# Sums of weights in DRAM issued two per step, and tile pools at new addresses

## The chip, the cores and the metric

The kernel runs on one core of a Trainium2 chip. PE (TensorE) does the matmuls, ACT (ScalarE) and DVE (VectorE) the work on single elements, POOL (GpSimd) and SP (SyncE) issue most of the transfers, which 16 DMA engines carry out. The metric is the time of one execution on the device in microseconds. An execution with a profile is a single one, and its time stands in the table below beside the span that the profile shows.

## The reference

One layer of a diffusion backbone: 512 latent tokens and 256 context tokens, 1,024 channels, all in fp32.

```python
mod_lat = silu(c) @ w_ada + b_ada              # six rows: sh1, sc1, ga1, sh2, sc2, ga2
z = modulate(x, g_norm1, sh1, sc1) @ w_in + b_in
x_a, b_a, c_a, q, k, v, r, lr_f, lr_b, gate_a, gate_b = split(z)
# ... the same projection of the context gives the first state of the scans
o = gla_bidir(q, k, v, g_f, g_b, s_f, s_b)     # gated linear attention, both directions, 4 heads
y_a = (b_a * conv3(c_a * x_a)) @ w_conv_out
y_b = (rmsnorm(o) * silu(r)) @ w_gla_out
y = sigmoid(gate_a) * y_a + sigmoid(gate_b) * y_b
x = x + ga1 * (y @ w_o)
x = x + ga2 * square(relu(modulate(x, g_norm2, sh2, sc2) @ w_up)) @ w_down
return rmsnorm(x, g_final)
```

## The kernel before, in words

Every large product is taken in three parts. An operand is split into a high part `h` and a low part `l`, both kept as fp32r, and `mm3` (line 132) issues high x high, high x low and low x high into the same PSUM tile. One weight tile of 128 x 1024 numbers gives 8 x 3 = 24 matmuls of 512 columns.

`weights` (line 121) brings such a tile: SP issues the load of a raw tile `r_`, ACT copies it to `h_` (the high part), DVE subtracts to get `l_`. There are four raw tiles (`NRAW`) and five of `h_` and `l_` each (`NW`). The class `Stream` walks through a plan of all weight tiles in the order of use (v, q, xa/c/b, ga, co, r, gb, go, wo, up, dn) and keeps up to three ahead. The names in the trace follow from it: `r_co`, `h_co`, `l_co` are the weights of the product `ps_co`. Of the two operands behind the arrow in a matmul's name, the first is the moving one and the second the stationary one: in ps_v, ps_y and the down projection the weights move, in all other products the activations do.

The main loop (line 923) runs over the 57 steps of `projections`. Beside each step it advances the attention of the four heads by one piece, then the sums, and from step 44 on (`MODS_FROM`) the second modulations, which load `wa` tiles into the same raw tiles. Then come the 16 steps of `gates` (r and gb), the products go and wo, and the MLP: 32 up tiles and 7 x 8 dn tiles. The seven products of the down projection use combinations of quarters of `w_down`, in the manner of Strassen and Winograd.

These combinations are the sums that the change is about. `weight_sums` (line 458) is a generator of 64 pieces of work on POOL. Each piece is two instructions: a COPY of one number of the latest low weight part to `tick`, which holds POOL back until that split is done, and a transfer from DRAM to DRAM into a tile `t`, either a plain copy of a quarter of `w_down` or of another `t`, or an accumulation onto `t`. In the order of issue: 16 copies, 16 accumulations, 8 copies from `t`, 8 accumulations, 8 copies, 8 accumulations. The first reader of a `t` is the third product of the down projection. `SUMS` says how many are drawn after step 0, step 1 and so on, the last entry standing for all later steps.

POOL's other work in that part of the program is small: two broadcasts of a bias (`vb`), clearing `lrf` and `lpb` for each head (lines 635, 636), and clearing and loading `acc` for the modulations. POOL issues in one order, so each of these stands behind the sums drawn before it. ACT, DVE and PE also keep the order in which a scheduler puts them.

The tile pools lie behind each other in SBUF in the order in which they are opened: `const`, `wp` (raw, high and low weights), `kp` (long-lived blocks, the projections' left or right operands `hh` and `hl`, `h2h`, `h2l`), `sp` (small columns) and `bp` (blocks of 512 numbers, among them `ogh`, `ogl`, `yh`, `yl`), in whose place `mp` comes later (`aph`, `apl`).

Of the kernel before, what the change touches and what calls it, by code (L numbers as in the profile page):

```python
# [8 lines left out]
F32 = mybir.dt.float32  # L9
# [6 lines left out]
P = 128  # L16
# [23 lines left out]
NBLK = 36  # L40
NKEEP = 16
MODS_FROM = 44
SUMS = (0, 1)
UP_ORDER = [16 * j + 4 * g + i for g in range(4) for j in range(2) for i in range(4)]
TABLES = "natural_log_exp_and_others"

# [2 lines left out]
def hybrid_block_kernel(  # L49
# [9 lines left out]
    w_up, w_down, b_in, b_ada, out = w_up[0], w_down[0], b_in[0], b_ada[0], out[0]  # L59

    const = es.enter_context(tc.tile_pool(name="const", bufs=1))
    wp = es.enter_context(tc.tile_pool(name="wp", bufs=NW))
    kp = es.enter_context(tc.tile_pool(name="kp", bufs=NKEEP))
    sp = es.enter_context(tc.tile_pool(name="sp", bufs=4))
    pp = es.enter_context(tc.tile_pool(name="pp", bufs=8, space=bass.MemoryType.PSUM))
    dp = es.enter_context(tc.tile_pool(name="dp", bufs=1, space=bass.MemoryType.DRAM))

# [36 lines left out]
    def raw_tile(name):  # L104
        return wp.tile([P, 1024], F32, tag="raw", name=name, bufs=NRAW)
# [4 lines left out]
    def split(src, hi, lo):  # L110
        act.copy(out=hi, in_=src)
        dve.tensor_tensor(out=lo, in0=src, in1=hi.bitcast(F32), op=ALU.subtract)
# [6 lines left out]
    latest = [None]  # L119

    def weights(name, src):

        raw = raw_tile("r_" + name)
        a, b = src.shape[1], src.shape[2]
        nc.sync.dma_start(out=raw.rearrange("p (a b) -> p a b", a=a), in_=src)
        hi = wp.tile([P, 1024], F32R, tag="hi", name="h_" + name)
        lo = wp.tile([P, 1024], F32R, tag="lo", name="l_" + name)
        split(raw, hi, lo)
        latest[0] = lo
        return hi.rearrange("p (a b) -> p a b", a=a), lo.rearrange("p (a b) -> p a b", a=a)  # L130
# [282 lines left out]
    mod_w[1] = [ada_raw(1, q) for q in range(2)]  # L413
    normalized(x_tok, r_x, 0, P)
    wq = weights("q0", cols(w_in, C_Q))
    key_weights(1)
    Engine.ordered = False
# [32 lines left out]

    t_sum = [[dp.tile([P, 2, 512], F32, tag=f"t{i}_{p}", name=f"t{i}_{p}") for p in range(NFF // 4)] for i in range(4)]
    tick = const.tile([1, 1], F32, name="tick")

    def quarter(j, hf, p):
        return rows(w_down, 16 * j + 2 * p, 512 * hf)

    def weight_sums():

        groups = range(NFF // 4)
        todo = [(i, p, quarter(0, i, p), False) for p in groups for i in range(2)]  # L460
        todo += [(i, p, quarter(i, 1, p), True) for p in groups for i in range(2)]
        for i, j, hf in ((2, 1, 1), (3, 1, 0)):
            todo += [(i, p, t_sum[(0, 2)[i - 2]][p], False) for p in groups]
            todo += [(i, p, quarter(j, hf, p), True) for p in groups]
        for i, p, src, add in todo:
            pinned(nc.gpsimd.tensor_copy(out=tick, in_=latest[0][0:1, 0:1].bitcast(F32)))
            pinned(nc.gpsimd.dma_start(out=t_sum[i][p], in_=src, **({"accum_op": ALU.add} if add else {})))  # L467
            yield

    def down_weights(n, p):  # L470

        if n in (2, 3, 5, 6):
            return weights("dn", t_sum[{2: 0, 3: 2, 5: 1, 6: 3}[n]][p])
        return weights("dn", quarter(*{0: (1, 0), 1: (0, 0), 4: (1, 1)}[n], p))
# [300 lines left out]
    def all_attention():  # L775
        for h in range(HEADS):
            yield from attention(h)
# [3 lines left out]
    def second_mods():  # L781
        yield from ada_sum(3)
        ps = psum("ps_ac")
        for k in range(KT):
            pe.matmul(ps[:, k:k + 1], ada[3][k // 4][:, (k % 4) * P:(k % 4 + 1) * P], ones[:, 0:1], start=True, stop=True)
        dve.tensor_copy(out=sh2, in_=ps[:, 0:KT])
        yield
        yield from ada_rows(4)
        for hf in range(2):
            g2 = blk("g2")  # L790
            nc.gpsimd.dma_start(out=g2, in_=g_norm2[0][hf * 512:(hf + 1) * 512].partition_broadcast(P))
            dve.scalar_tensor_tensor(out=ada[4][hf], in0=ada[4][hf], scalar=1.0, in1=g2, op0=ALU.add, op1=ALU.mult)
        yield from ada_rows(2)
# [110 lines left out]
    def gates():  # L904

        for j in range(KT):
            ps = project("r")
            rg = blk("rg")
            pinned(act.activation(out=rg, in_=ps, func=AF.Silu, bias=cb(40 + j)))
            pst = transposed("ps_ot", o_tok, j)  # L910
            dve.scalar_tensor_tensor(out=rg, in0=pst, scalar=ca(80 + j), in1=rg, op0=ALU.mult, op1=ALU.mult)
            og.append((blk(f"ogh_{j}", F32R), blk(f"ogl_{j}", F32R)))
            split(rg, *og[j])
            yield
        for j in range(KT):
            ps = project("gb")
            gb.append(kblk("gb"))
            pinned(act.activation(out=gb[j], in_=ps, func=AF.Sigmoid, bias=cb(56 + j)))
            yield
        pinned(nc.scalar.preload_act_table_set(TABLES))  # L920

    att, mods, sums = all_attention(), second_mods(), weight_sums()
    for i, _ in enumerate(projections()):
        next(att, None)
        for _ in range(SUMS[min(i, len(SUMS) - 1)]):
            next(sums, None)
# [3 lines left out]
        next(mods, None)  # L930
    for _ in gates():
        next(mods, None)
        next(sums, None)
    for _ in mods:
        pass
    for _ in sums:
# [291 lines left out]
```

## Time and profile before

| | |
|---|---|
| median of 3 runs | 1000.24 us (999.66 to 1001.4) |
| the profiled execution | 1002.8 us, span 1001.0 us |
| mean granted clock of PE | 0.989 of 2.4 GHz |
| PE busy | 963.0 us, 96% |
| DVE, ACT, POOL busy | 637.0, 487.8, 109.2 us |
| chain that ended last | PE 90%, DMA 4%, DVE 3% |
| DMA queue q1 (SP's and others' loads) | 41.4% of 16 engines, 123.89 MB |
| DMA queue q0 (POOL's transfers) | 15.1% of 16 engines, 35.43 MB |

The page gives for each engine the time in which it executed something, and the chain of waits follows the work that ended last back to its beginning. A matmul's shown duration overlaps the next one's; how fast PE works is therefore read from the starts, or from a piece of the chain (so many microseconds for so many matmuls without a break). The granted clock is 1.00 at 2.4 GHz and 0.50 at 1.2 GHz.

### The profile page before, as it was taken

To read this page: it belongs to the slowest core of one execution; us is meant where nothing else is said; L and a number is where in the kernel's file an instruction comes from. 1 tells how busy PE (TensorE), PEld (TensorE's weight loads), DVE (VectorE), ACT (ScalarE), POOL (GpSimd) and SP (SyncE) were. 2 spreads that over 40 slices of the span, in tenths; PEclk is the share of its full clock that TensorE was granted. 3 is DMA by queue.
4 is the path that set the end of the run, shared out by engine and by line. 5 is a ranking of instruction groups with operands and counts; after the bars stand their busy time and mean duration, and the time that the engine had idled before them with its cause. 6 is when DMAs were issued, how large, how long until landed. Compare 5 with 4: busy or idle time off the path is not lost.

```text
span 1001.0 us, 13478 instructions
## 1 busy us (share of the span) xinstructions
PE 963.0 (96%) x4999; PEld 783.9 (78%) x4999; DVE 637.0 (64%) x1076; ACT 487.8 (49%) x862; POOL 109.2 (11%) x195
## 2 busy tenths in 40 slices
PE   3999999999999998799989999999999999999996
PEld 2678888778888887688878888898888888888875
DVE  5366676887688767666547354776332225699896
ACT  4465454645655474533334432374444344655662
POOL 7001021222211131002220000000000000000000
PEclk9999999999999999899989999999999999999998
DMA  9893154787664666855987425237533334555561
GB/s 264 231 289 127 33 190 138 164 169 164 144 167 146 172 129 154 244 169 175 251 205 235 129 98 171 61 89 234 162 85 105 95 116 142 192 179 191 179 211 42
DMA packets 160241, 161.22 MB, mean 161 GB/s; under 512 B 7268, under 2 KB 126160, under 8 KB 159920
## 3 DMA queue, kind: packets, MB, share of 16 engines
q1 hardware_dynamic: 146672, 123.89, 41.4%
q0 software_dynamic: 12928, 35.43, 15.1%
q10 hardware_dynamic: 576, 1.05, 0.3%
q8 instruction: 39, 0.64, 0.3%
q14 instruction: 26, 0.21, 0.1%
HBM read 158.25 MB, written 35.65 MB: 194 GB/s over the span
## 4 chain that ended last, share of the span: by engine, by line
PE 90%; DMA 4%; DVE 3%; SPq 1%; ACT 1%; issue 1%; DVEq 0%; ACTq 0%
PE ps_up L81 16%; PE ps_da L81 7%; PE ps_v L81 7%; PE ps_b L81 4%; PE ps_y L81 4%; PE ps_c L81 4%; PE ps_db L81 4%; PE ps_go L81 4%; PE ps_xa L81 4%; PE ps_gb L81 4%; PE ps_co L81 4%; PE ps_r L81 4%; PE ps_ga L81 2%; PE ps_dc L81 2%; DMA r_co<-in_w_conv_out_dram 2%; PE ps_k L81 2%
## 5 line engine op out<-in xcount | busy, mean ns | idle before, releaser
L81 DVE TENSOR_TENSOR l_up<-r_up,h_up 128x1024 fp32r<-128x1024 f32 x32 | 39.2, 1224 | 84.8 <-ACT h_up L81 84.7
L81 PE MATMUL ps_up<-h2h,l_up 128*128 128x512 f32 x232 | 90.3, 389 | 0.0
L81 PE MATMUL ps_up<-h2l,h_up 128*128 128x512 f32 x232 | 90.3, 389 | 0.0
L81 PE MATMUL ps_up<-h2h,h_up 128*128 128x512 f32 x232 | 90.3, 389 | 0.0
L81 DVE TENSOR_TENSOR l_dn<-r_dn,h_dn 128x1024 fp32r<-128x1024 f32 x56 | 68.4, 1222 | 27.1 <-ACT h_dn L81 26.9
L81 ACT CAST h_up<-r_up 128x1024 fp32r<-128x1024 f32 x32 | 33.6, 1053 | 78.8 <-PE ps_up L81 67.9
L81 ACT CAST h_dn<-r_dn 128x1024 fp32r<-128x1024 f32 x56 | 58.7, 1048 | 16.1 <-PE ps_up L81 16.1
L81 ACT CAST aph<-ug 128x512 fp32r<-128x512 f32 x56 | 34.8, 621 | 58.8 <-PE ps_da L81 25.6
L81 DVE SCALAR_TENSOR_TENSOR acc<-wa,silu_c,acc 128x512 f32<-128x512 f32 x64 | 45.4, 747 | 8.4 <-DMA wa<-in_w_ada_dram 8.2
L81 PEld LDWEIGHTS ps_up<-h2l,h_up 128*128 128x128 f32 x232 | 43.5, 188 | 9.1
L81 PEld LDWEIGHTS ps_up<-h2h,l_up 128*128 128x128 f32 x232 | 43.5, 188 | 9.0
L81 PEld LDWEIGHTS ps_up<-h2h,h_up 128*128 128x128 f32 x232 | 43.5, 188 | 9.0
L81 DVE TENSOR_TENSOR apl<-ug,aph 128x512 fp32r<-128x512 f32 x56 | 38.6, 689 | 13.5 <-ACT aph L81 13.2
L467 POOL DMA_DIRECT2D t<-in_w_down_dram x48 | 42.7, 905 | 3.8 <-issue 3.8
L81 PE MATMUL ps_da<-h_dn,aph 128*128 128x512 f32 x96 | 37.9, 395 | 0.0
L81 PE MATMUL ps_da<-h_dn,apl 128*128 128x512 f32 x96 | 37.9, 395 | 0.0
L81 PE MATMUL ps_da<-l_dn,aph 128*128 128x512 f32 x96 | 37.9, 394 | 0.0
L81 PE MATMUL ps_co<-yah,h_co 128*128 128x512 f32 x64 | 26.5, 413 | 0.0
L81 PE MATMUL ps_r<-hh,h_r 128*128 128x512 f32 x64 | 26.4, 412 | 0.0
L81 PE MATMUL ps_v<-h_v,hh 128*128 128x512 f32 x64 | 26.0, 406 | 0.0
L81 PE MATMUL ps_r<-hh,l_r 128*128 128x512 f32 x64 | 25.8, 402 | 0.0
L81 PE MATMUL ps_r<-hl,h_r 128*128 128x512 f32 x64 | 25.7, 401 | 0.0
(464 smaller groups left out, 2794.5 us busy)
## 6 DMA issues: line engine op xcount, KB each, us to landing
t<-in_w_down_dram POOLq DMA_DIRECT2D x48, 512.0 KB, 7.6
wa<-in_w_ada_dram SPq DMA_DIRECT2D x32, 512.0 KB, 4.8
r_up<-in_w_up_dram SPq DMA_DIRECT2D x32, 512.0 KB, 4.1
r_dn<-t SPq DMA_DIRECT2D x32, 512.0 KB, 3.5
r_dn<-in_w_down_dram SPq DMA_DIRECT2D x24, 512.0 KB, 3.6
wa<-in_w_ada_dram SPq DMA_DIRECT2D x32, 256.0 KB, 5.1
t<-t POOLq DMA_DIRECT2D x16, 512.0 KB, 5.3
r_v<-in_w_in_dram SPq DMA_DIRECT2D x8, 512.0 KB, 5.2
```

What stands on the lines that cost most here:

```text
L81: ins = op(*args, **kwargs)
L467: pinned(nc.gpsimd.dma_start(out=t_sum[i][p], in_=src, **({"accum_op": ALU.add} if add else {})))
```

## The change

`SUMS` becomes (0, 1, 2): no sum after step 0, one after step 1, two after each later step until none is left. The loop over `gates` no longer draws any. The pool `sp` is opened before `wp`, a tile of 24 numbers at the end of `const` moves all later pools by 96 bytes, and a tile of 16 numbers (64 bytes) is put once between the high and the low weight parts. Everything else in the program stays, apart from line numbers.

```diff
-SUMS = (0, 1)
+PAD = 24
+SUMS = (0, 1, 2)
...
     const = es.enter_context(tc.tile_pool(name="const", bufs=1))
+    sp = es.enter_context(tc.tile_pool(name="sp", bufs=4))
     wp = es.enter_context(tc.tile_pool(name="wp", bufs=NW))
     kp = es.enter_context(tc.tile_pool(name="kp", bufs=NKEEP))
-    sp = es.enter_context(tc.tile_pool(name="sp", bufs=4))
...
         hi = wp.tile([P, 1024], F32R, tag="hi", name="h_" + name)
+        if latest[0] is None:
+            wp.tile([P, 16], F32, tag="gap", name="gap", bufs=1)
         lo = wp.tile([P, 1024], F32R, tag="lo", name="l_" + name)
...
     tick = const.tile([1, 1], F32, name="tick")
+    const.tile([P, PAD], F32, name="pad")
...
     for _ in gates():
         next(mods, None)
-        next(sums, None)
```

In the built programs the tiles start at these places, given as the address within a partition modulo 256 bytes (all the tiles concerned are multiples of 256 bytes long, so those of one kind share the place):

| | before | after |
|---|---|---|
| raw and high weights (`r_`, `h_`) | 32 | 0 |
| low weights (`l_`) | 32 | 64 |
| `kp` (`hh`, `hl`, `h2h`, `h2l`, ...) | 32 | 64 |
| `bp`, `mp` (`yah`, `ogh`, `yh`, `aph`, ...) | 160 | 64 |

Counted over the matmuls of 512 columns (without a few of the modulations), by the distance of the places of their two operands: before, 2,280 at distance 0 (v, q, xa, c, b, ga, r, gb, up) and 1,284 at 128 (co, go, y, the seven products of the down projection, k); after, about 1,252 at 0 and 2,312 at 64, two in three of nearly every stage, since `h_` is an operand of two of the three parts and `l_` of one.

On POOL, around the first tick on l_c, where the projections xa, c and b begin, the order was this (COPY is the tick, DMA the sum; the tile's first number is its place among the eight of a group):

```order
L466 COPY tick<-l_q 1x1
L467 DMA t_5_695<-in_w_down_dram 256x1x512
L466 COPY tick<-l_c 1x1
L467 DMA t_6_688<-in_w_down_dram 256x1x512
L635 MEMSET lrf 128x512
L636 MEMSET lpb 128x512
L466 COPY tick<-l_b 1x1
L467 DMA t_6_696<-in_w_down_dram 256x1x512
L466 COPY tick<-l_xa 1x1
L467 DMA t_7_689<-in_w_down_dram 256x1x512
```

Now the same place on POOL reads:

```order
L470 COPY tick<-l_c 1x1
L471 DMA t_3_694<-in_w_down_dram 256x1x512
L470 COPY tick<-l_c 1x1
L471 DMA t_4_687<-in_w_down_dram 256x1x512
L639 MEMSET lrf 128x512
L640 MEMSET lpb 128x512
L470 COPY tick<-l_b 1x1
L471 DMA t_4_695<-in_w_down_dram 256x1x512
L470 COPY tick<-l_b 1x1
L471 DMA t_5_688<-in_w_down_dram 256x1x512
L470 COPY tick<-l_xa 1x1
L471 DMA t_5_696<-in_w_down_dram 256x1x512
```

Each split now lets two sums go, and the clearing of `lrf` and `lpb` stands behind one more of them; 23 sums lie ahead of the first tick on l_c, where 12 did, so the 24th, an accumulation, stands where the 13th, a copy, stood.

Later on POOL, where the loads of ga give way to those of co and the second modulations start (`acc`), the order was:

```order
L751 DMA acc0_3831<-in_b_ada_dram 1x16x32
L751 DMA acc1_3832<-in_b_ada_dram 1x16x32
L466 COPY tick_714<-l_ga_3844 1x1
L467 DMA t2_4_702<-in_w_down_dram 256x1x512
L466 COPY tick_714<-l_co_3920 1x1
L467 DMA t2_5_703<-in_w_down_dram 256x1x512
L466 COPY tick_714<-l_co_3995 1x1
L467 DMA t2_6_704<-in_w_down_dram 256x1x512
```

Now the last sums on POOL stand on splits of xa and c, and `acc` comes after all of them:

```order
L470 COPY tick_715<-l_xa_3052 1x1
L471 DMA t3_6_713<-in_w_down_dram 256x1x512
L470 COPY tick_715<-l_c_3124 1x1
L471 DMA t3_7_714<-in_w_down_dram 256x1x512
L639 MEMSET lrf_3716 128x512
L640 MEMSET lpb_3717 128x512
L754 MEMSET acc0_3873 128x512
L754 MEMSET acc1_3874 128x512
L755 DMA acc0_3873<-in_b_ada_dram 1x16x32
```

No sum is left for the steps of ga, co, r and gb. On PE, DVE, ACT and SP the order is the same, row by row, as before.

## Rows read from the trace of the kernel before

**Rows 1.** The page's busy times, whole span

```profile
PE 963.0 (96%) x4999; PEld 783.9 (78%) x4999; DVE 637.0 (64%) x1076; ACT 487.8 (49%) x862; POOL 109.2 (11%) x195
```

**Rows 2.** Chain of waits, pieces at ps_gb, ps_go, ps_up (start us, us, what)

```profile
524.97 35.13 PE ps_gb L81 x155
...
569.99 35.09 PE ps_go L81 x151
...
689.84 40.35 PE ps_up L81 x178
```

**Rows 3.** PE's timeline in the ps_go steps (start us, us, what)

```profile
570.28 0.40 PE L81 MATMUL ps_go<-ogl,h_go 128*128 128x512 f32 x1
570.52 0.40 PE L81 MATMUL ps_go<-ogh,l_go 128*128 128x512 f32 x1
```

**Rows 4.** PE's timeline around 415 us (idle before and its releaser in brackets)

```profile
414.67 1.12 PE L81 MATMUL ps_sl<-qt,kt 128*64 128x64 f32 x16 [5.01 <-DVE kt L81]
...
416.32 0.63 PE L81 MATMUL ps_co<-yal,h_co 128*128 128x512 f32 x1
...
418.02 0.63 PE L81 MATMUL ps_co<-yah,l_co 128*128 128x512 f32 x1
```

**Rows 5.** PE's timeline, three more starts after idle time

```profile
386.44 0.69 PE L81 MATMUL ps_sl<-qt,kt 128*64 128x64 f32 x16 [1.76 <-DVE kt L81]
...
388.72 0.58 PE L81 MATMUL ps_s<-vcl,kwh 128*128 128x256 f32 x1 [1.28 <-DVE vcl L81]
...
504.65 0.80 PE L81 MATMUL ps_ar<-ah,ones_r 128*128 128x512 f32 x1 [2.81 <-ACT ah L81]
```

**Rows 6.** Windows: first and last of three stretches, PEclk before DMA share

```profile
388.15:391.56 3.41, 2.84 (x12) 2.84 (x13) 3.41 (x8) 1.15 (x5) 0.00 (x0) 0.50 0.24 65
...
504.20:511.03 6.83, 6.37 (x14) 4.70 (x15) 1.80 (x3) 0.92 (x2) 0.89 (x1) 0.50 1.10 278
```

**Rows 7.** The chain of waits, 370 to 420 us

```profile
374.10 8.63 DMA r_co<-in_w_conv_out_dram
...
397.49 13.14 DMA r_co<-in_w_conv_out_dram
```

**Rows 8.** DMA issues of the page, KB each, median us to landing

```profile
r_ga<-in_w_in_dram SPq DMA_DIRECT2D x8, 512.0 KB, 4.5
```

**Rows 9.** DMA queues of the whole span: packets, MB, share of 16 engines

```profile
q1 hardware_dynamic: 146672, 123.89, 41.4%
q0 software_dynamic: 12928, 35.43, 15.1%
```

**Rows 10.** DMA queues, 180 to 290 us

```profile
q0 software_dynamic: 4083, 7.87, 43.4%
q1 hardware_dynamic: 16438, 8.29, 27.5%
```

**Rows 11.** DMA queue q0 and its issues, 472 to 516 us

```profile
q0 software_dynamic: 2128, 4.20, 50.2%
...
t<-in_w_down_dram POOLq DMA_DIRECT2D x8, 512.0 KB, 9.8
```

**Rows 12.** Windows: an early stretch, DMA share before GB/s

```profile
92.00:164.00 72.00, 72.00 (x478) 60.71 (x477) 47.92 (x99) 30.41 (x68) 7.55 (x13) 1.00 0.24 78
```

**Rows 13.** POOL and DVE timelines: two ticks, vb, lrf and their first readers

```profile
124.09 0.60 POOL L827 DMA_DIRECT2D vb<-in_b_in_dram  x1
...
164.43 1.04 POOL L466 COPY tick<-l_c 1x1 f32<-1x1 f32 x1 [30.32 <-DVE l_c L81]
...
165.96 0.55 POOL L635 MEMSET lrf<- 128x512 f32 x1
...
292.04 0.17 POOL L466 COPY tick<-l_c 1x1 f32<-1x1 f32 x1 [3.43 <-DVE l_c L81]
...
132.29 0.69 DVE L81 TENSOR_TENSOR v<-ps_v,vb 128x512 f32<-128x512 f32 x1
...
177.02 0.42 DVE L81 TENSOR_TENSOR lrf<-lrf,lpf 128x256 f32<-128x256 f32 x1
```

## The prediction

> **What bounds the kernel now.** I read the page's busy times first. PE is busy for 963.0 of 1001.0 us and no other engine for more than 637.0 [rows 1], so the time is the sum of what PE executes, how fast matmul follows matmul, and the few places where PE stands still. I then took these two apart, because the change touches both, one with its DRAM sums and the other with its addresses.
>
> The speed of the stream is read in long unbroken pieces of the chain of waits. At ps_gb 155 matmuls take 35.13 us, 226.6 ns each; at ps_up 178 take 40.35 us, 226.7 ns each; at ps_go 151 take 35.09 us, 232.4 ns each [rows 2]. All are 512 columns wide at full clock. What sets ps_go apart in the table of addresses is that its two operands stand 128 bytes apart modulo 256, while those of ps_gb and ps_up stand at the same place. In ps_go single distances reach 240 ns, between the starts at 570.28 and 570.52 [rows 3]. At half clock four distances take 1.70 us, 425 ns each [rows 4], so half of that, some 213 ns, is what 512 columns would take at full clock with nothing lost between them.
>
> The idle places are read on PE's timeline. From 20 to 970 us only four idle spells exceed 1 us: 1.76 and 1.28 us before 386.44 and 388.72, 5.01 us before 414.67 and 2.81 us before 504.65 [rows 4, 5], in all 10.86 us. PE waits there for DVE or ACT, but neither is the cause. The chain goes back from them to r_co, which takes 8.63 and 13.14 us to land [rows 7]; ACT, which splits weights and serves attention in one fixed order, stands before h_co and everything behind it stands too. The load r_ga, of equal size, lands in a median of 4.5 us [rows 8]. Beside the stalls the granted clock falls to 0.50 in three stretches of 3.41 to 6.83 us [rows 6]. In that state a matmul takes 427 instead of 232 ns. Seven matmuls in the second stretch and 14 in the third lose some 0.195 us each, 4.1 us; of the first, 3.41 us long, at most half is lost, 1.7. That makes 5.8 us.
>
> **The change part by part.** First the sums. Nothing is added: the same 64 copies and accumulations run, and PE, DVE, ACT and SP keep their order word for word. Only POOL's order changes. From the second projection step on each step issues two, so of 64 the last comes in about the 33rd step, near 292 us by the times of before, and none in the steps of co, r and gb. DMA q0 spends 15.1% of 1001.0 us on some 64 transfers [rows 9], 2.36 us of all 16 engines each, and in 472 to 516 us, where eight accumulations stand, 50.2% [rows 11]. There they share the engines with the loads of r and gb. If that is what makes r_co and r_gb late, the loads come nearer to the 4.5 us of r_ga, the four spells and the clock behind them go, and 10.86 + 5.8 = 16.7 us are gained. What is late next is the ring of four raw buffers, which the modulation weights (wa) share from step 44 on; that stays, and I leave 2.7 us to it. I take −14 us; the bounds are 0 and −16.7.
>
> The cost of the sums where they go: between 180 and 290 us q0 and q1 already take 43.4% and 27.5% [rows 10]. The last 41 sums will stand on the 21 ticks from l_c at 164.43 to l_c at 292.04 [rows 13], 41 × 2.36 = 97 us of transfer, and with 27.5% of these 127.6 us, 35 us, for the loads: 132 us of transfer in 128 us. The loads of that stretch are issued some 20 us ahead of their split, and that queue ahead hides a delay of 5 to 10 us per load; I cost it at nothing. Without that cover it is rival 4. The sums on l_v and l_q, 23 instead of 12, fall in or before a stretch of 72 us with a DMA share of 0.24 [rows 12], where 55 us are free for 11 × 2.36 = 26 us more; also nothing. Behind the longer first burst stand the second vb and, two sums further back each time, the memsets of lrf and lpb. Vb is issued at 124.09 and read from 132.29 on; lrf is cleared at 165.96 and read at 177.02 [rows 13]. One or two sums more in front (about 1 us of POOL's issue each) fit into 8 and 11 us, so nothing here either.
>
> Second the addresses. Of 3,564 wide products 2,280 had both operands at the same place modulo 256 and 1,284 were 128 apart; now about 1,252 are at the same place and 2,312 are 64 apart. No product of the kernel before is 64 apart, so the price is bounded. From below it is 213 ns, the bare columns; from above 240 ns, the longest single distance of ps_go [rows 3]; the rows nearest on either side, at distances 0 and 128, are 226.7 and 232.4 ns. I take 226.7, because 64 is nearer to a full match in phase than the half period, where single distances swing; this is the weakest choice of the sum. With it the 1,284 lose 5.7 ns each, −7.3 us. Each nanosecond of error on the 2,312 is worth 2.3 us, so the ends are 2,312 × (213 − 226.7) − 7.3 = −39 us and 2,312 × (240 − 226.7) − 7.3 = +23 us.
>
> The sum: the profiled execution took 1002.8 us, 1.8 more than its span. 1002.8 − 14 − 7.3 = 981.5 us. The median of the runs shown is 1000.24, 2.56 lower, which makes 979 us.
>
> **The rivals.** (1) Distance costs as such: the 2,312 products run at the 232.4 ns of ps_go. For it speaks that this is the only unequal distance that a row shows. Against it, that 128 is the farthest that two places can be. Then (2,312 − 1,284) × 5.7 = +5.9 us stand against −14: 992 us.
>
> (2) The lost time between matmuls is a meeting of two readers at the same place, and 64 bytes apart they don't meet. For it: 226.7 is 14 ns above the bare columns even where nothing waits. Against: at 128 apart it got worse. At 213 ns it gives 2,312 × −13.7 − 7.3 = −39 us, with the sums 947 us. The Trainium skill has a gap of its own for this ("TensorE: Matmul & The Clock Gate", section "Back-to-back issue gap"): a matmul of 512 columns follows the last after 518 cycles, 216 ns. The trace doesn't agree, at 226.6 and 232.4 ns [rows 2]; by the page's figure on the 2,312 this rival would read 954 us.
>
> (3) Addresses don't matter to PE, and ps_go is slower for another reason, its left operand's age or DVE's traffic say. Then only the sums count, −14 us: 986 us. The Trainium skill says so: in "SBUF — State Buffer", section "Who interferes with whom", PE has two independent read ports and never waits on anyone. Against it stand two products of the same shape, engine and clock that differ by 5.8 ns [rows 2].
>
> (4) The moved sums starve the loads. An accumulation costs more than the mean: 50.2% of 44 us for eight is 2.8 us [rows 11]. A load costs 41.4% of 1001.0 us × 0.52 of 123.89 MB, 1.75 us [rows 9]. Two accumulations and a load take 7.35 us, a step takes 127.6 us / 21 = 6.1, and over 12 steps with accumulations 15 us are short. Uncovered, that and a clock spell of some 2 us return as stalls: 979 + 17 = 996 us. Against it: the loads' lead is longer than that.
>
> (5) The co and r loads are late from the raw ring and the wa loads, not the sums. For it: r_co at 374.10 is issued only when its buffer falls free. Against: its 8.63 us from issue to landing are past that point [rows 7]. Half of the stalls stay: 986 us.
>
> (6) The slower side: 64 apart, every distance is as long as the longest of ps_go. One mechanism, a clash of the two operand streams in 2,312 products, at 240 ns: +23 − 14 = 1009 us. It decides from the pitch at which 2,312 × (p − 226.7) exceeds 14 + 7.3, that is 235.9 ns. For it: 128 showed that a distance can cost, and nothing bounds it at 64. Against: even ps_go averages 232.4.
>
> **How the numbers follow.** Forecast (973 to 985 us) 0.40; rival 1 0.13; rival 2 0.15; rival 3 0.08; rival 4 0.07; rival 5 0.06; rival 6 0.11. The predicted time is 979 us. Rival 2 reaches to 947 and I leave out its lower half; rivals 1 and 4 can end near 1000, and of rival 6 the lower part is taken in: 950 to 1003 us. A measurement of this kernel can't tell 0.2%, 2 us, from no change. Slower by more: rival 6 and a little of rivals 1 and 4, 0.14. Within: 0.08 from the edges of the same. Faster: 0.78.
>
> **What would show it.** In the changed profile: no idle spell of PE over 1 us between 380 and 510 us, granted clock 1.00 throughout that stretch, r_co and r_gb landing in 4 to 6 us, and no `t` issue by POOL after some 300 us. The sums term is wrong if idle spells stay at co and gb, or new ones stand between 160 and 300 us behind r_xa, r_c or r_b. The address term is read in the pieces of ps_gb, ps_go and ps_up: about 227 ns in all three is the forecast, 232 rival 1, under 220 rival 2, unchanged by stage rival 3, 236 and more rival 6. The prediction is wrong as a whole if the long pieces' pitch lies outside 222 to 230 ns.

## The result and the profile after

The changed kernel takes 995.52 us (median of 19 runs, 994.3 to 1000.83) against 1001.45 us for the kernel before (19 runs, 999.06 to 1006.05). The ratio is 0.994, with a 95% interval of 0.9928 to 0.9953. That is 6 us faster; I had forecast 979 us, a gain of 21 us; the range of 950 to 1003 us holds the time.

The profiled execution took 1000.83 us, the longest of the 19, with a span of 999.1 us. The page of the changed kernel, with the line of busy times, the granted clock in 40 slices, and the chain by engine:

```profile
PE 966.6 (97%) x4999; PEld 780.7 (78%) x4999; DVE 637.3 (64%) x1076; ACT 487.8 (49%) x862; POOL 107.5 (11%) x195
...
PEclk9999999989999999999999999999999999999999
...
PE 87%; DMA 7%; DVE 3%; ACT 1%; SPq 1%; issue 1%; POOL 0%; DVEq 0%; ACTq 0%; POOLq 0%
```

PE is busy 3.6 us longer than before [rows 1] although the span is shorter, and the ninth slice of the clock has an 8: the loss sits elsewhere now.

First the stretch of co, r and gb. This is the DMA view from 370 to 420 us: queues (packets, MB, share of 16 engines), then the issues of r_co with their median time to landing.

```profile
q1 hardware_dynamic: 8362, 6.93, 46.4%
...
q0 software_dynamic: 64, 0.00, 0.1%
...
r_co<-in_w_conv_out_dram SPq DMA_DIRECT2D x8, 512.0 KB, 4.0
```

The same view of the kernel before:

```profile
q0 software_dynamic: 1216, 3.15, 31.0%
...
r_co<-in_w_conv_out_dram SPq DMA_DIRECT2D x7, 512.0 KB, 8.6
```

The sums are gone from q0, and r_co lands in a median of 4.0 us, where before it was 8.6 and two of its loads took 8.63 and 13.14 us [rows 7]. The four idle spells of [rows 4, 5] have no counterpart, and the clock stays at 1.00 from 220 to 995 us.

Second, the chain of waits near 214 us (start us, us, what), and the timelines of ACT and PE behind it:

```profile
178.12 32.50 DMA r_c<-in_w_in_dram
...
210.70 1.05 ACT h_c L82
...
211.83 1.23 DVE l_c L82
...
213.66 0.62 DVE kt L82
...
214.42 1.12 PE ps_sl L82 x16
```

```profile
210.70 1.04 ACT L82 CAST h_c<-r_c 128x1024 fp32r<-128x1024 f32 x1 [10.87 <-DMA r_c<-in_w_in_dram]
```

```profile
214.42 1.12 PE L82 MATMUL ps_sl<-qt,kt 128*64 128x64 f32 x16 [4.21 <-DVE kt L82]
```

A load of r_c, issued at 178.12, takes 32.50 us to land. ACT stands before h_c for it for 10.87 us, DVE behind ACT, and PE has nothing to do for 4.21 us until kt is there. It is the same chain of events as the stall at co before, 200 us earlier. The windows view shows what follows (the clock stands before the DMA share), and beside it the whole stretch of the doubled sums; the DMA queues of that stretch come behind.

```profile
213.55:220.38 6.83, 5.96 (x28) 4.82 (x29) 6.83 (x14) 3.37 (x8) 3.70 (x7) 0.50 0.83 267
164.00:290.00 126.00, 121.28 (x673) 97.53 (x671) 91.39 (x171) 68.71 (x139) 50.15 (x80) 0.97 0.94 230
```

```profile
q0 software_dynamic: 5917, 18.82, 62.7%
q1 hardware_dynamic: 19919, 10.04, 30.9%
```

The clock is at 0.50 for 6.83 us, and q0 and q1 together take 93.6% of the engines from 164 to 290 us, with 62.7% for the sums. Before they took 43.4% and 27.5% in nearly the same stretch [rows 10]. How the two queues share the engines while r_c is under way is seen from 178 to 186 us:

```profile
q0 software_dynamic: 696, 1.34, 90.4%
q1 hardware_dynamic: 696, 0.35, 21.6%
```

Both moved the same number of packets, 696, but those of the loads are much smaller, so SP's queue got 0.35 MB in 8 us. At that rate one load of 512 KB takes some 12 us (an estimate from these two lines), and several were waiting: the loads of r_b and r_xa that follow took 26.7 and 21.6 us. With the old addresses (sums_only, 174 to 182 us) the counts are 701 and 699.

Third, the speed of the stream, from pieces of the chain at gb, go and the down projection, and behind them the down projection of the kernel before:

```profile
524.94 35.25 PE ps_gb L82 x154
...
569.86 28.15 PE ps_go L82 x123
...
879.93 18.29 PE ps_dc L82 x78
```

```profile
879.80 18.37 PE ps_dc L81 x79
```

These are 228.9, 228.9 and 234.5 ns for a matmul, in what follows its pitch, the mean time from one start to the next. Before, gb ran at 226.6, go at 232.4 [rows 2] and the down projection at 232.5. Of the three only go has become faster. Over all distances from start to start of consecutive wide matmuls of one product (those under 300 ns), the mean rises from 229.4 to 231.3 ns.

Where the time went can be read by stage, from the first start of each stage on PE's timeline to that of the next (us). Each column is the one profiled execution of its kernel, which for the changed kernel and for places_only is the longest of its runs:

| stage | before | changed | sums_only | places_only | aligned | paced |
|---|---|---|---|---|---|---|
| from 8 us on: first modulations, keys, v (to the keys of the context) | 88.6 | 91.0 | 88.7 | 88.8 | 86.6 | 88.2 |
| context keys, rest of v, q | 76.4 | 78.6 | 76.7 | 77.5 | 77.3 | 76.7 |
| xa, c, b | 171.2 | 179.7 | 178.6 | 172.7 | 179.1 | 171.2 |
| ga, co, r | 175.9 | 158.8 | 157.9 | 180.3 | 157.5 | 158.7 |
| gb, go, y | 136.5 | 136.5 | 136.5 | 136.5 | 134.2 | 134.2 |
| up | 177.2 | 178.6 | 177.2 | 178.6 | 177.2 | 177.2 |
| down | 158.3 | 159.5 | 158.3 | 159.5 | 154.6 | 154.6 |

The columns behind the second are the experiments below. In ga, co and r the change gains 17.1 us; in xa, c and b it loses 8.5, of which 1.5 are there with the new addresses alone and 7.4 with the new sums alone. The addresses add 1 us or so to each of up and down.

### The profile page after: what moved, and what is told of

The parts are those of the page before. It is cut to its first block, busy times and chain, and to the rows that moved or that the text cites. A ratio compares the mean times of both kernels' runs of the same rounds, so it can differ in the third digit from the quotient of the medians.

```text
span 999.1 us, 13441 instructions
## 1 busy us (share of the span) xinstructions
PE 966.6 (97%) x4999; PEld 780.7 (78%) x4999; DVE 637.3 (64%) x1076; ACT 487.8 (49%) x862; POOL 107.5 (11%) x195
## 4 chain that ended last, share of the span: by engine, by line
PE 87%; DMA 7%; DVE 3%; ACT 1%; SPq 1%; issue 1%; POOL 0%; DVEq 0%; ACTq 0%; POOLq 0%
PE ps_up L82 16%; PE ps_da L82 7%; PE ps_co L82 5%; PE ps_ga L82 5%; PE ps_y L82 5%; PE ps_db L82 5%; PE ps_r L82 4%; PE ps_go L82 4%; PE ps_gb L82 4%; PE ps_b L82 4%; PE ps_v L82 4%; PE ps_c L82 3%; PE ps_xa L82 3%; DMA r_c<-in_w_in_dram 3%; PE ps_dc L82 2%; PE ps_dd L82 2%
## 5 line engine op out<-in xcount | busy, mean ns | idle before, releaser
L82 PE MATMUL ps_b<-hh,h_b 128*128 128x512 f32 x64 | 26.8, 419 | 0.0
L754 POOL MEMSET acc<- 128x512 f32 x8 | 4.1, 526 | 204.4 <-DVE yl L82 101.0
L82 PE MATMUL ps_b<-hl,h_b 128*128 128x512 f32 x64 | 26.1, 408 | 0.0
L82 PE MATMUL ps_b<-hh,l_b 128*128 128x512 f32 x64 | 25.8, 403 | 0.0
```

The source lines that it names most:

```text
L82: ins = op(*args, **kwargs)
L754: nc.gpsimd.memset(acc[hf], 0.0)
```

## The experiments

The theories were, from the result: the sums and the addresses act apart and add up (A), against the addresses not mattering at all (B). Then, whether the cost of an address lies in the change of place from part to part or in the distance (A1, A2), and what makes the new stall (C, D). E to H belong to the last runs on the distance and stand in their expectations.

**sums_only**: the pools of before with

```diff
-SUMS = (0, 1)
+SUMS = (0, 1, 2)
...
     for _ in gates():
         next(mods, None)
-        next(sums, None)
```

> The new SUMS with the pools at their old addresses. Theory A (sums and addresses act apart: the sums remove the stalls at co and gb, the new addresses make the matmuls follow each other more slowly): pitch as before (226.7 ns at gb and up, 232.4 at go and the down projection), no idle spell of PE over 1 us between 380 and 510 us, perhaps one of about 4 us near 214 us as in the changed kernel; 985 to 992 us. Theory B (addresses don't matter to PE; the changed kernel gained only what its sums give): the same as the changed kernel, 995 us.

It takes 991.77 us (6 runs, 990.81 to 994.17), a ratio of 0.9898 (0.9877 to 0.9918) to before, and is thus faster than the whole change. The pitch is that of before: 226.7 ns at gb, 232.3 at go, 232.4 in the down projection. Its chain, PE's timeline, and its DMA queues from 164 to 290 us:

```profile
173.73 32.68 DMA r_c<-in_w_in_dram
```

```profile
210.21 1.12 PE L81 MATMUL ps_sl<-qt,kt 128*64 128x64 f32 x16 [4.80 <-DVE kt L81]
```

```profile
q0 software_dynamic: 6292, 19.54, 65.9%
q1 hardware_dynamic: 20603, 10.39, 32.4%
```

No idle spell over 1 us is left between 380 and 510 us. The late load of r_c and the stall behind it are there with the old addresses too, so the doubled sums bring them. Theory B, which needed 995, fails; theory A's 985 to 992 us holds at its upper edge.

**places_only**: the changed kernel with the old sums.

```diff
-SUMS = (0, 1, 2)
+SUMS = (0, 1)
...
     for _ in gates():
         next(mods, None)
+        next(sums, None)
```

> The new addresses with the old SUMS. Theory A: pitch as in the changed kernel (229 ns at gb, go and up, 234 at v, y and the down projection), stalls at co and gb as before; 6.5 us more than before, about 1008 us. Theory B: no difference from before, 1001 us.

It takes 1004.69 us (12 runs, 1002.23 to 1012.04), a ratio of 1.0035 (1.0015 to 1.0055), so the addresses alone make the kernel slower, by 3.5 us by that ratio (the medians are 2.7 us apart) rather than the 6.5 that I had expected. The time lies between theory A's 1008 us and theory B's 1001; the pitch decides for A, as the wide products have that of the changed kernel (means of 229.1 at gb, 234.4 in the down projection). PE's timeline has the old stalls, with the fourth longer than before:

```profile
389.71 0.69 PE L82 MATMUL ps_sl<-qt,kt 128*64 128x64 f32 x16 [2.51 <-DVE kt L82]
...
391.98 0.58 PE L82 MATMUL ps_s<-vcl,kwh 128*128 128x256 f32 x1 [1.14 <-DVE vcl L82]
...
418.18 1.12 PE L82 MATMUL ps_sl<-qt,kt 128*64 128x64 f32 x16 [4.04 <-DVE kt L82]
...
512.04 0.79 PE L82 MATMUL ps_ar<-ah,ones_r 128*128 128x512 f32 x1 [5.50 <-ACT ah L82]
```

The two parts alone, -10.2 and +3.5 us, make -6.7, and together they make -6. Within their intervals they add up.

**aligned**: the changed kernel without the gap, so that every tile concerned stands at 0 modulo 256.

```diff
         hi = wp.tile([P, 1024], F32R, tag="hi", name="h_" + name)
-        if latest[0] is None:
-            wp.tile([P, 16], F32, tag="gap", name="gap", bufs=1)
         lo = wp.tile([P, 1024], F32R, tag="lo", name="l_" + name)
```

> The changed kernel without the 64-byte tile, so that all weights, kp, bp and mp stand at 0 modulo 256. Theory A: every wide product at 226.7 ns, 13 us less than the changed kernel, 982 us (a few us more if the stall near 214 us is there). Theory B: as the changed kernel, 995 us.

It takes 984.88 us (5 runs, 983.04 to 987.63), a ratio of 0.9829 (0.9805 to 0.9852); theory A's 982 us and a few more for the stall is met. The stall near 210 us is there (5.02 us). The pieces at gb, go and the down projection:

```profile
524.86 27.66 PE ps_gb L82 x122
...
569.77 27.20 PE ps_go L82 x120
...
879.94 5.67 PE ps_dc L82 x25
```

That is 226.7, 226.7 and 226.8 ns, in all three what gb and up had before [rows 2]. Taking 64 bytes out of the program is worth 11 us.

**uniform64**: aligned with a tile of 64 bytes in front of kp, so weights stand at 0 and everything else at 64.

```diff
+    kp.tile([P, 16], F32, tag="gap", name="gap", bufs=1)
     bp = tc.alloc_tile_pool(name="bp", bufs=NBLK)
```

> All weights (high and low) at 0, kp, bp and mp at 64 modulo 256, so that all three parts of a product are 64 bytes apart and none changes the distance. Theory A1 (what costs is the change of place from one matmul to the next, as in the changed kernel, where the parts alternate between distance 0 and 64): 226 to 228 ns in all stages, 982 us. Theory A2 (the distance of 64 bytes itself costs): 229 ns or more in all stages, above 234 where the weights move, 996 to 1003 us.

994.17 us (6 runs, 992.65 to 994.84). The pieces at gb and the down projection:

```profile
524.84 29.30 PE ps_gb L83 x128
...
879.93 12.13 PE ps_dc L83 x52
```

228.9 ns where activations move and 233.3 where weights move. No part changes its distance here, and the cost is there all the same: theory A1 falls as the only cause. A2 holds for the mechanism, with numbers a little lower than it had (233.3 instead of over 234 ns, 994 instead of 996 to 1003 us).

A1 is not gone altogether. In the changed kernel one product in three stands at distance 0. If each product kept the price of its own distance, the pitch would be 228.2 ns where activations move (two at 228.9, one at 226.7) and 231.1 where weights move (two at 233.3, one at 226.7). Measured are 228.9 and 234.5 ns, so some 0.7 and 3.4 ns, an estimate from these pieces, go with the change of place from part to part; no run tests this by itself. In the down projection's timeline the mean from start to start is 235.5 ns onto a product with l_dn, 238.0 from it to the next, and 229.7 between the two products with h_dn.

**uniform192, uniform32, uniform96**: the same tile with 48, 8 and 24 numbers, one run each.

```diff
-    kp.tile([P, 16], F32, tag="gap", name="gap", bufs=1)
+    kp.tile([P, 48], F32, tag="gap", name="gap", bufs=1)
```

> As uniform64, with kp, bp and mp at 192 instead of 64, so that the sign of the distance between moving and stationary operand is reversed. Theory E (what counts is by how much the moving operand's place lies ahead of the stationary one's): the numbers of uniform64 change sides, 233.3 ns at up, gb and go, 228.9 at v, y and the down projection; 995 to 999 us. Theory F (what counts is whether weights or activations move): 228.9 at up, gb and go, 233.3 at v, y and down; 994 us.

> As uniform64 with kp, bp and mp at 32. If the cost grows with the distance (0 at 0, 2.2 and 6.6 ns at 64): about 1 ns more than aligned where activations move and 3 ns where weights move, 989 us. If any distance costs the same: as uniform64, 994 us.

> As uniform64 with kp, bp and mp at 96, which completes the steps of 32 bytes: moving minus stationary operand is 96 where activations move and 160 where weights move. The pitches so far are 226.7 at 0, 233.3 at 32, 228.9 at 64, 232.4 at 128, 233.3 at 192 and at 224. Theory G (only multiples of 64 bytes ahead have a steady order, other distances share the worst value): 233.3 in all stages, 1002 us. Theory H (a smooth curve around 128): 230 to 233 ns, 997 us. A pitch under 226.7 anywhere would refute that the same place is best.

They took 996.96, 1002.22 and 1004.78 us. A single run has no interval, so the pitch counts here and not the time; the stall near 210 us is in all three, and in uniform96 it is the longest, at 6.92 us. Pieces at gb and the down projection, of uniform192:

```profile
524.98 32.44 PE ps_gb L83 x139
...
879.91 16.94 PE ps_dc L83 x74
```

The numbers of uniform64 have changed sides, 233.4 at gb and 228.9 in the down projection: theory E holds, it is the moving operand's place less the stationary one's that counts, not which of them is the weight. Of uniform32:

```profile
524.90 33.83 PE ps_gb L83 x145
...
879.95 18.20 PE ps_dc L83 x78
```

and of uniform96:

```profile
524.92 35.23 PE ps_gb L83 x151
...
880.20 17.81 PE ps_dc L83 x76
```

Both are at 233.3 ns at gb; the down projection at 233.3 and 234.3. For 32 neither expectation holds (989 us if the cost grew with the distance, 994 if any distance cost the same): the cost doesn't grow with the distance, and it isn't the same at every distance. Theory G's number, 233.3 ns, is right for 96 and 1 ns short for 160; the order at multiples of 64 bytes that it supposed isn't there, since 192 takes 233.4. In one table, by moving less stationary place modulo 256:

| distance | 0 | 32 | 64 | 96 | 128 | 160 | 192 | 224 |
|---|---|---|---|---|---|---|---|---|
| ns for 512 columns | 226.7 | 233.3 | 228.9 | 233.3 | 232.4 | 234.3 | 233.4 | 233.3 |

(0 and 128 as in [rows 2], the others from uniform64 and these runs; 160, 192 and 224 are the down projection of uniform96, the gb of uniform192 and the down projection of uniform32.)

**paced**: aligned, with the sums two per step up to the first tick on l_c, then one per step while they are accumulations and two while they copy from t.

```diff
-SUMS = (0, 1, 2)
+SUMS = (0, 1) + 11 * (2,) + 9 * (1,) + 4 * (2,) + 8 * (1,) + 4 * (2,) + 8 * (1,) + (0,)
```

> All pools at 0 modulo 256 as in aligned; sums two per step up to the first tick on l_c, then one per step while they are accumulations and two per step while they are copies from t, all done with the last ga step. Theory C (the stall near 210 us comes from two sums per step, which fill the DMA engines beside the loads from 164 us on): no idle spell over 1 us between 150 and 520 us, granted clock 1.00 there, r_c in at most 15 us; 7 us less than aligned, 977 to 978 us. Theory D (it comes from the early burst of 23 sums on l_v and l_q, which this run keeps): stall and time as in aligned, 985 us.

979.07 us (4 runs, 976.54 to 979.69), a ratio of 0.9766 (0.9742 to 0.979) to before: faster than both kernels, and 6 us faster than aligned. The windows from 164 to 290 us, the queues there, and the one spell near 385 us:

```profile
164.00:290.00 126.00, 125.50 (x733) 101.67 (x731) 100.08 (x194) 71.73 (x148) 31.81 (x52) 1.00 0.78 183
```

```profile
q0 software_dynamic: 4379, 12.15, 45.2%
q1 hardware_dynamic: 21453, 10.81, 32.5%
```

```profile
385.43 0.39 PE L82 MATMUL ps_s<-vcl,kwh 128*128 128x256 f32 x1 [0.92 <-DVE vcl L82]
```

The clock is 1.00, q0 takes 45.2% instead of 62.7%, and the stage of xa, c and b lasts 171.2 us as before the change. The gain on aligned is 5.8 us where 7 was expected. Theory C holds; the early burst, kept here, isn't the cause (D falls). The last sums stand in the ga steps, early enough for co and gb.

**no_sums**: aligned without any sum; the down projection loads quarters of w_down instead.

```diff
-        return weights("dn", t_sum[{2: 0, 3: 2, 5: 1, 6: 3}[n]][p])
+        return weights("dn", quarter(0, 0, p))
...
-        for i, p, src, add in todo:
+        for i, p, src, add in todo[:0]:
```

> As aligned, but with all 64 sums left out; the down projection loads quarters of w_down in their place (same sizes, other numbers), so the output isn't the reference's. The least that the sums can cost: if C and D are right that the sums only cost the stall, 977 to 978 us; if they also slow other things (start, splits), less, 970 to 976 us.

It computes something else than the reference, since the sums are left out. It takes 974.75 us (4 runs, 974.37 to 974.93), within the 970 to 976 us of the expectation's second case: the sums of paced cost some 4 us more than none, though no stall over 1 us is left in their stretch.

## Why the prediction was wrong

The direction was right; the size was not. Step by step:

1. **The stalls at co and gb come from the sums and go with them.** Right. I had put the gain at -14 us with a bound of -16.7. In ga, co and r it was -17.1 in the changed kernel and -18.0 in sums_only, so the 2.7 us left to the raw buffers were not needed and the bound itself was a little tight. Rival 5, that half of the stalls would stay for want of raw buffers, is refuted: the ring and the wa loads are unchanged and the spells are gone.

2. **The sums cost nothing where they go, because loads are issued some 20 us ahead.** This step failed, and what rival 4 names came in: the stage of xa, c and b lost 7.4 us (sums_only against before), 4.80 of them idle and most of the rest at the half clock behind. I had weighed the transfers as a mean over 128 us and let the lead of the loads cover the rest. But from 178 to 186 us, with two accumulations per step, the two queues moved equally many packets, which left the small packets of the loads 0.35 MB of 1.69, and r_c took 32.50 us, 10.87 more than its lead. Rival 4 had the mechanism and more than twice the price (17 us); that its 996 us lies beside the measured 995.52 is luck, as it had the addresses gain 7.3 us.

3. **2,312 products 64 bytes apart run at 226.7 ns.** This step failed and is the larger part of the error. Those 2,312 are not of one kind: where activations move the distance is 64, where weights move it is 64 the other way, 192, and the two have different prices. The products of the changed kernel, their three parts together, run at 228.9 ns where activations move and at 234.5 where weights do, part of which goes, by the estimate at uniform64, with the change of place between parts. With the mean pitch 1.9 ns up over 3,564 products the term is +6.9 us by the trace instead of -7.3; by places_only it is +3.5 (the interval of its ratio is 1.5 to 5.5 us). Rival 1, 232.4 at any distance, was nearest with +5.9, but by luck: no stage of the three read above runs at 232.4. The prediction's reason, that 64 is closer to a match in phase than 128, had no row behind it; 32 is closer still and costs 6.6 ns.

4. **Rival 3, that addresses don't matter to PE,** for which I had named the Trainium skill ("SBUF — State Buffer", section "Who interferes with whom"), is refuted by uniform192 and uniform64: only a gap differs, and gb takes 233.4 or 228.9 ns. Rivals 2 and 6 are refuted by the table of distances; nothing under 226.6 or over 234.5 ns was seen in any long piece.

So -14, 0 and -7.3 should have read -17, +7.4 and +3.5 to +6.9. That sum runs from -6.1 to -2.7 us, and the -6 that was measured is at its better end. That paced takes 979 us, the time forecast, isn't the change's merit: it has what the prediction assumed, sums that starve no load and all products at 226.7 ns, and the change has neither.

What stays open: the addresses cost 3.5 us by the times and 6.9 by the pitch, and uniform32 too is only 17.3 us above aligned where the means of its distances from start to start, 233.2 against 227.4 ns, would make it 20.7; no run tells what takes up the rest. The profiled execution of the changed kernel is 5 us above its median, 4.6 us of it against before in the first two stages, where places_only shows 1.3; no run tells why. And why the pitch depends on the distance, and on its change from part to part, was not tried, only that it does.

## What to carry to other kernels

Where PE is the bound, read the pitch of long pieces of the chain for each product and compare it with the places of the two operands modulo 256: here the same place for both was best, and a pad of some bytes alone moved the kernel between 984.88 us and, in a single run, 1004.78 us, 2%. Look at the order of the two as well: the moving operand 64 bytes ahead cost 2.2 ns, 64 behind 6.6. When background transfers are moved, sum them and the loads for each stretch they go to, and spread them where the total comes near the stretch's length, with the heavier kinds thinner. A mean over the whole stretch doesn't bound the latest load; compare the packets of the two queues where the densest transfers stand.

## What the hardware showed unexpectedly

The pitch of 512-column matmuls is not a smooth function of the distance of the operands' addresses: 32 bytes cost as much as 224 (233.3 ns), 64 less (228.9), and the sign counts (192 takes 233.4). When the place changes from product to product, as in the down projection of the changed kernel, the mean is 234.5 ns although a third of the products stand at distance 0. And a load of 512 KB that lands in 4 to 5 us in the medians of [rows 8] and of r_co here took 32.1 to 35.5 us at the same step in all seven kernels with the doubled sums. From 164 to 290 us q0 and q1 held 94% to 98% of the DMA engines there, two thirds of it on POOL's queue; from 178 to 186 us of the changed kernel each queue moved 696 packets, but POOL's carried 1.34 MB and SP's 0.35 MB.
